# A hybrid decoder trunk: the inversion's small products in eight groups, Silu on ScalarE, and the norm's two steps moved

## The chip, the cores and the metric

The kernel runs on one core of one Trainium2 chip. The metric is the device time of one execution in microseconds (us). A core has five engines that run side by side and wait for each other by semaphores: TensorE (PE, matrix products; PEld is its weight load), VectorE (DVE), ScalarE (ACT), GpSimd (POOL) and SyncE (SP, which starts DMA transfers). Products land in PSUM, which has eight banks here called by tags; everything else is in SBUF.

## The reference

A trunk of DEPTH = 2 layers over 512 tokens of width 1024. Cut to what matters:

```python
for l in range(DEPTH):
    h = modulate(x, norm_ffn1[l], sh1, sc1)              # RMSNorm, scale, shift
    x = x + 0.5 * (1 + g1) * swiglu(h, ffn1_w1[l], ffn1_w3[l], ffn1_w2[l])
    h = modulate(x, norm_mix[l], sh2, sc2)
    x = x + (1 + g2) * token_mix(h, ...)                 # gated delta rule and MLA side by side
    h = modulate(x, norm_ffn2[l], sh3, sc3)
    x = x + 0.5 * (1 + g3) * swiglu(h, ffn2_w1[l], ffn2_w3[l], ffn2_w2[l])

def rms_norm(x, gain):
    return x * rsqrt(mean(x * x, -1) + EPS) * gain

def gated_deltanet(qkv, z, ...):
    q, k, v = split(silu(causal_dwconv(qkv, conv_w)))    # q, k: l2_norm per head
    ...
    t_inv = triangular_solve(eye + m, eye)               # m strictly lower, one per chunk and head
    ...
    return rms_norm(o, out_gain) * silu(z)

def mla(q_lat, kv_lat, ...):
    q = rms_norm(q_lat, q_lat_gain) @ w_q_up             # q_lat: 384 wide, kv_lat: 256 wide
    kv = rms_norm(kv_lat, kv_lat_gain) @ w_kv_up
    ...
```

Eight heads of width 128 in both mixers. The kernel works in chunks of 128 tokens, so per layer there are 8 x 4 = 32 triangular matrices of 128x128 to invert.

## The kernel before

Everything is held transposed: features on the 128 partitions, tokens along the free axis. A projection in float32 is made of three products in the faster fp32r format (`mm3`, L123): the high part of the weight by the high part of the activation, high by low, and low by high. A weight slab of 128x1024 comes in by DMA (`raw`), ACT casts it to the high part (`whi`, L119), and DVE subtracts to get the low part (`wlo`, L120). A **k-step** is three products of 128x128 by 512 columns; a **unit** is one slab, eight k-steps into one PSUM tile `acc`, and what is done with the result.

The mixer (`mix`) keeps a list of such units. Wherever a chain of small dependent work runs, `fill(n)` (L159) puts n k-steps of the queued units between its steps, so that PE has something to do. `FILL_INVERT`, `FILL_DELTA` and others say how many after which step. The order of the instructions on each engine is fixed when the program is built, by a list scheduler that goes by the program's order and by which instructions it takes to be ready; afterwards each engine runs its list strictly in order.

Places that the change and the prediction touch:

- `conv` (L498): the causal convolution of a head's q, k or v on ACT (L503) and DVE (L506), then Silu as a tanh on ACT (L508) and a DVE product (L509). Its result is twice the Silu; factors that make up for this are in `gdn_tail` (`4.0 * EPS`, `self.ogh`) and in `mix` (`nh`).
- `gdn_units` (L695): the units of a head's q, v and z. The z unit has its own tanh (L711) and DVE product (L713), which reads the `acc` tile.
- `latent_units` (L801): five units for the latents of MLA. Each squares its result (L811, into a `cv` buffer) and adds it (L815); the last unit of each kind then sums over the partitions by four products with a matrix of ones into an `sm` tile, and DVE makes the mean of it (L826).
- `invert` (L617): the 32 matrices at once. Each is cut in 32x32 blocks. DVE transposes the diagonal blocks (L629) and inverts them by 31 steps of substitution (L635, L637), in seven parts, each followed by 12 k-steps. Then L642 and L643 transpose the result to `xd` and `yd`; the tag `L` has five buffers, and `yd` gets its place in SBUF from those. Then come the **small products**: from the 32x32 inverses the 64x64 ones, from these the 128x128 ones, by products of 32x32 (160 per layer) and of 64x64 (64 per layer) in plain float32, each of which the profile shows as two records, 448 in all. They come in four stretches, with 8 k-steps behind each of the first three. The results are taken out of PSUM (`sm`, `sc`) by DVE and ACT copies.
- `gdn_chunk` and `gdn_tail` (L783): the delta rule itself and its output norm, which takes its root by `rsqrt`.
- `rsqrt` (L313): with a table, a Sqrt on ACT, a reciprocal and one Newton step on DVE; without, a first guess by integer arithmetic and three Newton steps, all on DVE.
- `norm_scale` (L328) makes an RMSNorm's factor in two steps: products with ones and the root; then a product that broadcasts the factor over the partitions (into `po`). `norm_apply` (L356) makes the next activations of it.
- `close` (L379) ends each half step: the output projection's slabs and their residual (L376), and on the way the sum of squares (`norm_square`, L301, whose L310 and L311 keep the running sum in `g`). The last four slabs are done once for the first 256 tokens (PSUM tag `acc`) and once for the second 256 (`sc`). The first half's norm is taken a step further after the residual of slabs 1 and 3 of the second half (`NORM_AT`). Its slabs have 8 k-steps after the mixer and up to 8 in the feed-forward parts, the last piece of whose inner width has 6.

Of the kernel before, what the change touches and what calls it, by code (L numbers as in the profile page):

```python
# [11 lines left out]
AF = mybir.ActivationFunctionType  # L12
# [27 lines left out]

FILL_INVERT = (12, 12, 12, 12, 12, 12, 12, 8, 8, 8)
FILL_DELTA = ((0, 2, 2), (2, 2, 2), (2, 2, 2), (2, 2, 2))
# [31 lines left out]
class Trunk:  # L74
    def __init__(self, ctx, tc, aps):
        self.tc = tc
        self.nc = tc.nc
        self.ap = aps
        self.sb = ctx.enter_context(tc.tile_pool(name="sb", bufs=1))
        self.ps = ctx.enter_context(tc.tile_pool(name="ps", bufs=1, space=bass.MemoryType.PSUM))  # L80
        self.count = 0
        self.pin = False
        self.units, self.body, self.ahead = [], None, None
        self.queue = []

    def order(self, i):
# [72 lines left out]
    def fill(self, n):  # L159

        for _ in range(n):
            while True:
                if self.body is None:
                    if not self.units:
                        return
                    load, body = self.units.pop(0)
                    self.body = body(self.ahead or load())
                    self.ahead = self.units[0][0]() if self.units else None
                if next(self.body, 0) != 0:
                    break  # L170
                self.body = None

    def fill_all(self):
        while self.units or self.body:
            self.fill(1)

    def hacts(self):
# [150 lines left out]
    def norm_scale(self, cols):  # L328
# [8 lines left out]
        nc.vector.tensor_scalar(var, ps[:, :, 0], 1.0 / D, EPS, ALU.mult, ALU.add)  # L337
        self.rsqrt(rn, var, True)
        yield
# [39 lines left out]
    def close(self, get, acts, gate, finish, spare=(), ahead=None):  # L379
# [15 lines left out]
        for (a, b), tag in zip(HALVES if ws else (), ("acc", "sc")):  # L395
            for m, s in zip(range(late, KT), ws):
                ps = self.p(tag)
                self.proj(ps, s, acts, (a, b))
                self.residual(m, ps, gate, (a, b))
                norm = finish(m, (a, b))  # L400
                if norms and m - late in NORM_AT:
                    next(norms[0], None)
                if norm is not None:
                    norms.append(norm)
# [92 lines left out]

    def conv(self, ps, vec, tile_index, out):  # L498

# [4 lines left out]
        for j in range(3):  # L504
            s = 3 - j
            nc.vector.scalar_tensor_tensor(acc[:, s:], ps[:, :SEQ - s], w[j], acc[:, s:], ALU.mult, ALU.add)  # L506
        th = self.t("cv", [P, SEQ])
        nc.scalar.activation(th, acc, AF.Tanh, scale=0.5)  # L508
# [108 lines left out]
    def invert(self, mall, tt):  # L617
# [13 lines left out]
        for j in range(B - 1):  # L631
# [6 lines left out]
            if j % 5 == 4:  # L638
# [6 lines left out]
        x64 = [self.t("O", [P, 16, 64]) for _ in range(2)]  # L645
        QUADS = [(slice(16 * i, 16 * i + 16), 16 * i, slice(a * B, (a + 1) * B), slice((a + 1) * B, (a + 2) * B), i, a)
                 for a in (0, 2) for i in range(2)]
        tags = ("sm", "sc")
        for ns, n0, sa, sb_, i, a in QUADS:
            ps = self.p(tags[i], [P, 16, B])  # L650
            for n in range(16):
                self.mm(ps[sb_, n, :], mall[sa, n0 + n, sb_], xd[sa, n0 + n, :], start=True, stop=True)
            nc.vector.tensor_copy(pq[sb_, ns, :], ps[sb_])
        for b in range(4):
            bs = slice(b * B, (b + 1) * B)
            nc.scalar.copy(tt[bs, :, bs], yd[bs])
        for i in range(2):
            ns = slice(16 * i, 16 * i + 16)
            nc.gpsimd.memset(x64[i][0:B, :, B:], 0.0)
            nc.scalar.copy(x64[i][0:B, :, 0:B], xd[0:B, ns, :])  # L660
            nc.scalar.copy(x64[i][B:2 * B, :, B:], xd[B:2 * B, ns, :])
        yield
        for ns, n0, sa, sb_, i, a in QUADS:
            if a == 0:
                ps3 = self.p(tags[i], [P, 16, B])
                for n in range(16):
                    self.mm(ps3[sb_, n, :], yd[sb_, n0 + n, :], pq[sb_, n0 + n, :], start=True, stop=True)
                nc.scalar.activation(x64[i][sb_, :, 0:B], ps3[sb_], AF.Copy, scale=-1.0)
        for ns, n0, sa, sb_, i, a in reversed(QUADS):
            ps2 = self.p(tags[i], [P, 16, B])  # L670
            for n in range(16):
                self.mm(ps2[sa, n, :], pq[sb_, n0 + n, :], yd[sb_, n0 + n, :], start=True, stop=True)
            nc.scalar.activation(tt[sa, ns, sb_], ps2[sa], AF.Copy, scale=-1.0)
        yield
        p2 = [self.t("O", [P, 16, 64]) for _ in range(2)]
        for i in range(2):
            for q in range(2):
                ps = self.p(tags[q], [P, 8, 64])
                for n in range(8):
                    m = 16 * i + 8 * q + n  # L680
                    self.mm(ps[64:, n, :], mall[0:64, m, 64:], x64[i][0:64, 8 * q + n, :],
                                     start=True, stop=True)
                nc.vector.tensor_copy(p2[i][64:, 8 * q:8 * q + 8, :], ps[64:])
        yield
        for i in range(2):
            for q in range(2):
                ps2 = self.p(tags[q], [P, 8, 64])
                m0 = 16 * i + 8 * q
                for n in range(8):
                    self.mm(ps2[0:64, n, :], p2[i][64:, 8 * q + n, :], tt[64:, m0 + n, 64:],  # L690
                                     start=True, stop=True)
                nc.scalar.activation(tt[0:64, m0:m0 + 8, 64:], ps2[0:64], AF.Copy, scale=-1.0)


    def gdn_units(self, l, h, vec, st):  # L695
# [4 lines left out]
        def qv(i, w):  # L700
            if i == 0:
                st["qv"] = self.t("O", [P, 2, SEQ])
            ps = self.p("acc")
            yield from self.proj_steps(ps, w, acts)
            self.conv(ps, vec, (h, 16 + h)[i], st["qv"][:, i, :])

        def z(w):
            ps = self.p("acc")
            yield from self.proj_steps(ps, w, acts)
            zt = self.t("cv", [P, SEQ])  # L710
            nc.scalar.activation(zt, ps, AF.Tanh, scale=0.5)  # L711
            st["z2"] = self.t("c3", [P, SEQ])
            nc.vector.scalar_tensor_tensor(st["z2"], zt, 1.0, ps, ALU.add, ALU.mult)  # L713

# [67 lines left out]

    def gdn_tail(self, st):  # L783

        nc = self.nc
        ssq, osb, z2 = st["ssq"], st["osb"], st["z2"]
        a, m = st["sso"], self.t("som", [P, NT])
        nc.vector.tensor_scalar(ssq, ssq, 4.0 * EPS, EPS * P, ALU.add, ALU.mult)
# [7 lines left out]
        nc.vector.scalar_tensor_tensor(z2, ot, self.ogh, z2, ALU.mult, ALU.mult)  # L796
        o = self.t("O", [P, 2, SEQ], F32R)
        self.split(o[:, 0, :], o[:, 1, :], z2)
        st["o"] = (o[:, 0, :], o[:, 1, :])

    def latent_units(self, l, vec, ms, out):  # L801
# [5 lines left out]
        def unit(i, w):  # L807
# [196 lines left out]
    def mix(self, l, vec, gate, finish, ws, ahead):  # L1004
# [21 lines left out]
        for h in range(2):  # L1026
            self.conv(pp[1 + h], vec, 8 + h, kT[h])
        for h in range(2, HEADS):
# [3 lines left out]
            self.key_system(l, gt, h - 2, kT[h - 2], mall)  # L1032
            self.conv(ps, vec, 8 + h, kT[h])
        heads = [{} for _ in range(HEADS)]
# [12 lines left out]
        nh = gt["nh"]  # L1047
        nc.vector.tensor_scalar(nh, gt["ssk"], 0.25, EPS, ALU.mult, ALU.add)
        rs = self.t("s1", [P, NI])
        self.rsqrt(rs[:], nh[:])  # L1050
        nc.vector.tensor_mul(nh, nh, rs)
        self.ogh = self.t("ogh", [P, 1])
        nc.vector.tensor_scalar(self.ogh, vec[:, V_OG:V_OG + 1], 0.5, None, ALU.mult)
        tt = self.t("A", [P, NI, P])
# [18 lines left out]
        for h in range(HEADS):  # L1073
            prep = self.gdn_prep(l, h + 1, gt, kT[h + 1], heads[h + 1]) if h + 1 < HEADS else iter(())
            for c in range(NT):
                for i, _ in enumerate(self.gdn_chunk(h, c, gt, kT[h], tt, heads[h])):
# [4 lines left out]
                    self.fill(FILL_DELTA[c][i])  # L1081
            tail = self.gdn_tail(heads[h])
            next(tail)
# [319 lines left out]
```

## Time and profile before

| | |
|---|---|
| median of 3 runs | 2811.39 us (2811.04 to 2812.45) |
| profiled execution | 2812.29 us |
| its span in the profile | 2810.4 us |
| PE busy | 2761.9 us, 98% |
| DVE busy | 1736.9 us, 62% |
| ACT busy | 1130.3 us, 40% |
| POOL busy | 156.4 us, 6% |
| DMA | 339.2 MB, mean 121 GB/s |

Times in the profile are in us from the start of the span, unless they are marked ns. A group row names the source line, engine, operation, output tile, inputs and count. A wait row names who waited for whom, the total, the number of times and the longest. The granted clock (PEclk) is the share of the full TensorE clock, 1.00 at most; the profile gives it in windows of 3.41 us. A busy PE is not the same as a PE at its pace: a small product and a product at half the clock both count as busy.

### The profile page before, as it was taken

What the parts mean: (1) busy time and instruction counts of PE and PEld (TensorE: products, weight loads), DVE (VectorE), ACT (ScalarE), POOL (GpSimd) and SP (SyncE); (2) the same over time, 40 slices, a digit from 0 to 9 for tenths busy, and PEclk for the clock granted to TensorE, in tenths of its full rate; (3) what the DMA queues carried; (4) which work ended last, traced back from release to release, by engine and by line L of the source; (5) the groups of instructions that cost most, each with busy time, mean ns of one, the idle gap of its engine ahead of it and who ended that gap; (6) DMA issues with size and microseconds to landing.
All of it is one profiled execution on the core that took longest, in us unless ns stands there. A gap on an engine that the chain in (4) does not pass through costs nothing. (4 is left out here: it accounts for less than half of the span.)

```text
span 2810.4 us, 38435 instructions
## 1 busy us (share of the span) xinstructions
PE 2761.9 (98%) x14648; PEld 2338.5 (83%) x14648; DVE 1736.9 (62%) x3677; ACT 1130.3 (40%) x2343; POOL 156.4 (6%) x238
## 2 busy tenths in 40 slices
PE   7999999999999999999999999999999999999999
PEld 6888888788888788888888888887888888988888
DVE  6555569867668755543456554797766786653333
ACT  3322255445546534222342222544555564432322
POOL 0000003000001010000000000130000111000000
PEclk9999999899999999999999999999999999999999
DMA  7556433222122343643336663332222223443332
GB/s 275 184 185 200 153 108 108 83 64 79 59 91 65 117 165 113 201 144 98 99 97 194 192 198 116 112 106 66 76 83 77 71 79 109 143 135 98 98 94 94
DMA packets 103720, 339.20 MB, mean 121 GB/s; under 512 B 11760, under 2 KB 14448, under 8 KB 103536
## 3 DMA queue, kind: packets, MB, share of 16 engines
q1 hardware_dynamic: 101088, 332.03, 37.2%
q10 hardware_dynamic: 2448, 4.72, 0.4%
q8 instruction: 115, 1.88, 0.3%
q14 instruction: 69, 0.57, 0.1%
HBM read 321.50 MB, written 15.20 MB: 120 GB/s over the span
## 5 line engine op out<-in xcount | busy, mean ns | idle before, releaser
L119 ACT CAST whi<-raw 128x512 fp32r<-128x512 f32 (+1 forms) x834 | 484.9, 611 | 1131.1 <-PE acc L92 535.2
L120 DVE TENSOR_TENSOR wlo<-raw,whi 128x512 fp32r<-128x512 f32 (+1 forms) x834 | 573.4, 708 | 244.6 <-ACT whi L119 236.6
L92 PE MATMUL acc<-hhi,whi 128*128 128x512 f32 (+1 forms) x1648 | 648.3, 394 | 3.2 <-DVE c L713 1.7
L92 PE MATMUL acc<-hlo,whi 128*128 128x512 f32 (+1 forms) x1648 | 628.0, 381 | 1.5 <-POOL hlo L370 1.5
L92 PE MATMUL acc<-hhi,wlo 128*128 128x512 f32 (+1 forms) x1648 | 628.6, 382 | 0.0
L92 PEld LDWEIGHTS acc<-hhi,wlo 128*128 128x128 f32 x1648 | 312.9, 190 | 59.8 <-DVE wlo L1230 0.4
L92 PEld LDWEIGHTS acc<-hhi,whi 128*128 128x128 f32 x1648 | 313.6, 191 | 53.2 <-DVE c L713 2.5
L92 PEld LDWEIGHTS acc<-hlo,whi 128*128 128x128 f32 x1648 | 314.2, 191 | 51.7 <-POOL hlo L370 2.5
L92 PE MATMUL acc<-O,whi 128*128 128x512 f32 x1088 | 335.8, 390 | 0.0
L92 PE MATMUL sc<-hhi,whi 128*128 128x512 f32 (+1 forms) x712 | 272.8, 383 | 0.0
L92 PE MATMUL sc<-hhi,wlo 128*128 128x512 f32 (+1 forms) x712 | 272.5, 383 | 0.0
L92 PE MATMUL sc<-hlo,whi 128*128 128x512 f32 (+1 forms) x712 | 272.3, 382 | 0.0
L92 PEld LDWEIGHTS acc<-O,whi 128*128 128x128 f32 x1088 | 203.5, 188 | 41.6
L428 DVE TENSOR_TENSOR g<-g,sc 128x512 f32<-128x512 f32 x87 | 59.8, 688 | 261.6 <-PE sc L92 256.8
L92 PE MATMUL acc<-O,wlo 128*128 128x512 f32 x544 | 211.9, 390 | 0.0
L376 DVE SCALAR_TENSOR_TENSOR M<-acc,gate,M 128x512 f32<-128x512 f32 (+1 forms) x112 | 77.5, 692 | 197.9 <-PE acc L92 191.4
L92 PE MATMUL acc<-A,whi 128*128 128x512 f32 x640 | 197.1, 389 | 0.0
L256 DVE SCALAR_TENSOR_TENSOR L<-L,L 128x1024 f32<-128x1024 f32 x142 | 169.4, 1218 | 0.2 <-DMA L<-in_ada_w 0.2
L92 PEld LDWEIGHTS sc<-hhi,wlo 128*128 128x128 f32 x712 | 134.2, 188 | 27.4 <-DVE wlo L120 1.3
L92 PEld LDWEIGHTS sc<-hlo,whi 128*128 128x128 f32 x712 | 134.0, 188 | 26.0
L92 PEld LDWEIGHTS sc<-hhi,whi 128*128 128x128 f32 x712 | 134.1, 188 | 25.8
L92 PEld LDWEIGHTS acc<-A,whi 128*128 128x128 f32 x640 | 120.1, 188 | 25.0
(373 smaller groups left out, 3725.2 us busy)
## 6 DMA issues: line engine op xcount, KB each, us to landing
raw<-in_ffn_w SPq DMA_DIRECT2D x236, 512.0 KB, 3.6
L<-in_ada_w SPq DMA_DIRECT2D x142, 512.0 KB, 4.6
raw<-in_w_in SPq DMA_DIRECT2D x108, 512.0 KB, 3.6
raw<-in_ffn_w SPq DMA_DIRECT2D x32, 384.0 KB, 3.2
raw<-in_w_branch_a SPq DMA_DIRECT2D x16, 512.0 KB, 3.5
raw<-in_w_branch_b SPq DMA_DIRECT2D x16, 512.0 KB, 3.6
raw<-in_w_out SPq DMA_DIRECT2D x16, 512.0 KB, 3.5
spill<-M SPq DMA_DIRECT2D x16, 256.0 KB, 2.0
```

The costliest lines, as they stand in the source:

```text
L92: i = self.nc.tensor.matmul(*a, **k)
L119: nc.scalar.copy(hi[:, s], raw[:, s])
L120: nc.vector.tensor_sub(lo[:, s], raw[:, s], hi[:, s].bitcast(F32))
L256: self.order(self.nc.vector.scalar_tensor_tensor(raw, raw, 1.0, self.condb, ALU.mult, ALU.mult, accum_out=mod[:, o:o + 1]))
L376: self.nc.vector.scalar_tensor_tensor(self.x[:, m, a:b], ps[:, a:b], gate[:, m:m + 1], self.x[:, m, a:b], ALU.mult, ALU.add)
L428: nc.vector.tensor_mul(s, s, ps3)
```

## The change

Five edits in one step.

1. The small products of the inversion come in nine groups with three k-steps between (eight gaps of 3, in place of three of 8). Within a group, products of two row blocks of the array alternate: blocks 0 and 2 in the first two groups, 1 and 3 in the next two; in the eighth group the upper and the lower half. The copies of `xd` and `yd` come behind the second group.
2. Silu is one ACT operation for q, v and z; the keys keep tanh and product. The factors 0.25, 0.5 and 4 that belonged to the doubled values go or move.
3. The root in `norm_scale` and in `gdn_tail` is taken without table, on DVE.
4. The latents' sum over the partitions is put on a list (`self.waiting`) and issued 14 k-steps later.
5. In `close` the two steps of the first half's norm come inside slab 1 and slab 3 of the second half, after 3/8 of its k-steps, rather than after the residual.

```diff
-FILL_INVERT = (12, 12, 12, 12, 12, 12, 12, 8, 8, 8)
+FILL_INVERT = (12, 12, 12, 12, 12, 12, 12) + (3,) * 8
...
                 if next(self.body, 0) != 0:
+                    self.count_down()
                     break
...
+    def count_down(self):
+        for w in list(self.waiting):
+            w[0] -= 1
+            if w[0] == 0:
+                self.waiting.remove(w)
+                w[1]()
...
-        self.rsqrt(rn, var, True)
+        self.rsqrt(rn, var, False)
...
-                self.proj(ps, s, acts, (a, b))
+                n = len(acts)
+                cut = 3 * n // 8 if norms and m - late in NORM_AT else n
+                self.proj(ps, s, acts, (a, b), range(cut))
+                if cut < n:
+                    next(norms[0], None)
+                    self.proj(ps, s, acts, (a, b), range(cut, n))
                 self.residual(m, ps, gate, (a, b))
                 norm = finish(m, (a, b))
-                if norms and m - late in NORM_AT:
-                    next(norms[0], None)
...
+        if not twice:
+            nc.scalar.activation(out, acc, AF.Silu)
+            return
         th = self.t("cv", [P, SEQ])
         nc.scalar.activation(th, acc, AF.Tanh, scale=0.5)
         nc.vector.scalar_tensor_tensor(out, th, 1.0, acc, ALU.add, ALU.mult)
...
-        for ns, n0, sa, sb_, i, a in QUADS:
+        for i, ns, n0 in halves:
             ps = self.p(tags[i], [P, 16, B])
             for n in range(16):
-                self.mm(ps[sb_, n, :], mall[sa, n0 + n, sb_], xd[sa, n0 + n, :], start=True, stop=True)
-            nc.vector.tensor_copy(pq[sb_, ns, :], ps[sb_])
+                for ra, rb in ((r0, r1), (r2, r3)):
+                    self.mm(ps[rb, n, :], mall[ra, n0 + n, rb], xd[ra, n0 + n, :], start=True, stop=True)
+            for rb in (r1, r3):
+                nc.vector.tensor_copy(pq[rb, ns, :], ps[rb])
...
+            yield
+        outs = []
+        for i, ns, n0 in halves:
+            ps2, ps3 = self.p(tags[i], [P, 16, B]), self.p(tags[i], [P, 16, B])
+            outs.append(ps2)
+            for n in range(16):
+                self.mm(ps3[r1, n, :], yd[r1, n0 + n, :], pq[r1, n0 + n, :], start=True, stop=True)
+                self.mm(ps2[r2, n, :], pq[r3, n0 + n, :], yd[r3, n0 + n, :], start=True, stop=True)
+            nc.scalar.activation(x64[i][r1, :, 0:B], ps3[r1], AF.Copy, scale=-1.0)
+            nc.scalar.activation(tt[r2, ns, r3], ps2[r2], AF.Copy, scale=-1.0)
+            yield
...
+        for i, ns, n0 in halves:
+            for n in range(16):
+                self.mm(outs[i][r0, n, :], pq[r1, n0 + n, :], yd[r1, n0 + n, :], start=True, stop=True)
+            nc.scalar.activation(tt[r0, ns, r1], outs[i][r0], AF.Copy, scale=-1.0)
+            yield
+        for q in range(2):
+            ps = self.p(tags[q], [P, 8, 64])
+            for n in range(8):
+                low(0, q, n, ps)
+            store_low(0, q, ps)
         yield
...
+        for q in range(2):
+            pl, ph = self.p(tags[q], [P, 8, 64]), self.p(tags[q], [P, 8, 64])
+            for n in range(8):
+                low(1, q, n, pl)
+                high(0, q, n, ph)
+            store_low(1, q, pl)
+            store_high(0, q, ph)
         yield
...
+        for q in range(2):
+            ps = self.p(tags[q], [P, 8, 64])
+            for n in range(8):
+                high(1, q, n, ps)
+            store_high(1, q, ps)
...
-            zt = self.t("cv", [P, SEQ])
-            nc.scalar.activation(zt, ps, AF.Tanh, scale=0.5)
-            st["z2"] = self.t("c3", [P, SEQ])
-            nc.vector.scalar_tensor_tensor(st["z2"], zt, 1.0, ps, ALU.add, ALU.mult)
+            st["z"] = self.t("c3", [P, SEQ])
+            nc.scalar.activation(st["z"], ps, AF.Silu)
...
-        self.rsqrt(m[:], a[:])
+        self.rsqrt(m[:], a[:], False)
...
-                s = self.p("sm", [P, NT, P])
-                for c in range(NT):
-                    self.mm(s[:, c, :], keep["sq"][:, c * P:(c + 1) * P], self.ones, start=True, stop=True)
                 which = 0 if i < QL else 1
-                n = (QL, KL)[which] * P
-                nc.vector.tensor_scalar(ms[:, which, :], s[:, :, 0], 1.0 / n, EPS, ALU.mult, ALU.add)
+                sq = keep["sq"]
+                self.waiting.append([14, lambda: mean(which, sq)])
```

`low` and `high` are the 64x64 products of the lower and upper half, `store_low` and `store_high` their copies out of PSUM (DVE and ACT); `mean` does what the lines taken from `unit` did.

More of the change, by code (lines that the diff above doesn't have):

```diff
@@ L84, in __init__ @@
         self.queue = []
+        self.waiting = []
     def order(self, i):
@@ L169, in fill @@
                 if next(self.body, 0) != 0:
+                    self.count_down()
                     break
                 self.body = None
+    def count_down(self):
[4 more added lines that the diff above has]
+                w[1]()
     def fill_all(self):
-        while self.units or self.body:
+        while self.units or self.body or self.waiting:
             self.fill(1)
+            if not (self.units or self.body):
+                self.count_down()
     def hacts(self):
@@ L495, in ffn, with conv @@
         down(2)
-    def conv(self, ps, vec, tile_index, out):
+    def conv(self, ps, vec, tile_index, out, twice):
         nc = self.nc
@@ L645, in invert @@
         x64 = [self.t("O", [P, 16, 64]) for _ in range(2)]
-        QUADS = [(slice(16 * i, 16 * i + 16), 16 * i, slice(a * B, (a + 1) * B), slice((a + 1) * B, (a + 2) * B), i, a)
-                 for a in (0, 2) for i in range(2)]
+        halves = [(i, slice(16 * i, 16 * i + 16), 16 * i) for i in range(2)]
+        r0, r1, r2, r3 = (slice(b * B, (b + 1) * B) for b in range(4))
         tags = ("sm", "sc")
-        for ns, n0, sa, sb_, i, a in QUADS:
+        for i, ns, n0 in halves:
             ps = self.p(tags[i], [P, 16, B])
@@ L651, in invert @@
             for n in range(16):
-                self.mm(ps[sb_, n, :], mall[sa, n0 + n, sb_], xd[sa, n0 + n, :], start=True, stop=True)
-            nc.vector.tensor_copy(pq[sb_, ns, :], ps[sb_])
[L654 to L661, printed above, removed]
@@ L662, in invert @@
-        yield
[L663 to L673, printed above, removed]
@@ L674, in invert @@
-        yield
[L675 to L692, printed above, removed]
+                for ra, rb in ((r0, r1), (r2, r3)):
+                    self.mm(ps[rb, n, :], mall[ra, n0 + n, rb], xd[ra, n0 + n, :], start=True, stop=True)
@@ new lines, in invert @@
+            for rb in (r1, r3):
+                nc.vector.tensor_copy(pq[rb, ns, :], ps[rb])
+            if i:
+                for b in range(4):
+                    bs = slice(b * B, (b + 1) * B)
+                    nc.scalar.copy(tt[bs, :, bs], yd[bs])
+                for j, js, _ in halves:
+                    nc.gpsimd.memset(x64[j][0:B, :, B:], 0.0)
+                    nc.scalar.copy(x64[j][r0, :, 0:B], xd[r0, js, :])
+                    nc.scalar.copy(x64[j][r1, :, B:], xd[r1, js, :])
@@ new lines, in invert, with low, high, store_low @@
+        p2 = [self.t("O", [P, 16, 64]) for _ in range(2)]
+        def low(i, q, n, ps):
+            self.mm(ps[64:, n, :], mall[0:64, 16 * i + 8 * q + n, 64:], x64[i][0:64, 8 * q + n, :], start=True,
+                    stop=True)
+        def high(i, q, n, ps):
+            m = 16 * i + 8 * q + n
+            self.mm(ps[0:64, n, :], p2[i][64:, 8 * q + n, :], tt[64:, m, 64:], start=True, stop=True)
+        def store_low(i, q, ps):
+            nc.vector.tensor_copy(p2[i][64:, 8 * q:8 * q + 8, :], ps[64:])
@@ new lines, in store_high @@
+        def store_high(i, q, ps):
+            m0 = 16 * i + 8 * q
+            nc.scalar.activation(tt[0:64, m0:m0 + 8, 64:], ps[0:64], AF.Copy, scale=-1.0)
+        for i, ns, n0 in halves:
[8 more added lines that the diff above has]
+            store_low(0, q, ps)
@@ L704, in qv @@
             yield from self.proj_steps(ps, w, acts)
-            self.conv(ps, vec, (h, 16 + h)[i], st["qv"][:, i, :])
+            self.conv(ps, vec, (h, 16 + h)[i], st["qv"][:, i, :], False)
         def z(w):
@@ L781, in gdn_chunk, with gdn_tail @@
         yield
-    def gdn_tail(self, st):
+    def gdn_tail(self, vec, st):
         nc = self.nc
-        ssq, osb, z2 = st["ssq"], st["osb"], st["z2"]
+        ssq, osb, z = st["ssq"], st["osb"], st["z"]
         a, m = st["sso"], self.t("som", [P, NT])
-        nc.vector.tensor_scalar(ssq, ssq, 4.0 * EPS, EPS * P, ALU.add, ALU.mult)
+        nc.vector.tensor_scalar(ssq, ssq, EPS, EPS * P, ALU.add, ALU.mult)
         nc.vector.scalar_tensor_tensor(a, a, 1.0 / P, ssq, ALU.mult, ALU.add)
-        self.rsqrt(m[:], a[:])
+        self.rsqrt(m[:], a[:], False)
         nc.vector.tensor_mul(osb, osb, m[:].unsqueeze(2).to_broadcast([P, NT, P]))
@@ L795, in gdn_tail @@
             self.tr(ot[:, c * P:(c + 1) * P], osb[:, c, :], self.ident)
-        nc.vector.scalar_tensor_tensor(z2, ot, self.ogh, z2, ALU.mult, ALU.mult)
+        nc.vector.scalar_tensor_tensor(z, ot, vec[:, V_OG:V_OG + 1], z, ALU.mult, ALU.mult)
         o = self.t("O", [P, 2, SEQ], F32R)
-        self.split(o[:, 0, :], o[:, 1, :], z2)
+        self.split(o[:, 0, :], o[:, 1, :], z)
         st["o"] = (o[:, 0, :], o[:, 1, :])
@@ L820, in unit, with mean @@
             if i in (QL - 1, QL + KL - 1):
-                s = self.p("sm", [P, NT, P])
-                for c in range(NT):
-                    self.mm(s[:, c, :], keep["sq"][:, c * P:(c + 1) * P], self.ones, start=True, stop=True)
                 which = 0 if i < QL else 1
-                n = (QL, KL)[which] * P
-                nc.vector.tensor_scalar(ms[:, which, :], s[:, :, 0], 1.0 / n, EPS, ALU.mult, ALU.add)
+                sq = keep["sq"]
+                self.waiting.append([14, lambda: mean(which, sq)])
+        def mean(which, sq):
+            s = self.p("sm", [P, NT, P])
+            for c in range(NT):
+                self.mm(s[:, c, :], sq[:, c * P:(c + 1) * P], self.ones, start=True, stop=True)
+            n = (QL, KL)[which] * P
+            nc.vector.tensor_scalar(ms[:, which, :], s[:, :, 0], 1.0 / n, EPS, ALU.mult, ALU.add)
         return [(lambda i=i: self.win(l, WLAT + i), lambda w, i=i: unit(i, w)) for i in range(QL + KL)]
@@ L1026, in mix @@
         for h in range(2):
-            self.conv(pp[1 + h], vec, 8 + h, kT[h])
+            self.conv(pp[1 + h], vec, 8 + h, kT[h], True)
         for h in range(2, HEADS):
@@ L1032, in mix @@
             self.key_system(l, gt, h - 2, kT[h - 2], mall)
-            self.conv(ps, vec, 8 + h, kT[h])
+            self.conv(ps, vec, 8 + h, kT[h], True)
         heads = [{} for _ in range(HEADS)]
@@ L1047, in mix @@
         nh = gt["nh"]
-        nc.vector.tensor_scalar(nh, gt["ssk"], 0.25, EPS, ALU.mult, ALU.add)
+        nc.vector.tensor_scalar(nh, gt["ssk"], 4.0 * EPS, None, ALU.add)
         rs = self.t("s1", [P, NI])
@@ L1051, in mix @@
         nc.vector.tensor_mul(nh, nh, rs)
-        self.ogh = self.t("ogh", [P, 1])
-        nc.vector.tensor_scalar(self.ogh, vec[:, V_OG:V_OG + 1], 0.5, None, ALU.mult)
         tt = self.t("A", [P, NI, P])
@@ L1081, in mix @@
                     self.fill(FILL_DELTA[c][i])
-            tail = self.gdn_tail(heads[h])
+            tail = self.gdn_tail(vec, heads[h])
             next(tail)
```

## The prediction

> **What bounds the kernel now.** I read the page first (busy shares, the chain of work that ended last), then the waits of TensorE (PE) alone, then tables of windows, and last the timeline of the few places where PE is not at its pace. The first fence is the pace (chain of waits), the second PE's waits: releaser, total us, times, longest.
>
> ```profile
> 2545.22 48.96 PE acc L92 x216
> ```
> ```profile
> PE sm L92 <- DVE cv L815: 7.8, 2, 3.9
> ...
> PE sm L92 <- DVE g L311: 5.5, 5, 1.1
> ...
> PE acc L92 <- DVE c L713: 1.7, 2, 0.9
> ```
> The third is windows: stretch, length, busy time (and instructions) of PE, PEld, DVE, ACT, POOL, then granted clock, DMA share, GB/s. The span comes first, then per layer the *long stage* (seven fills of 12 k-steps beside the substitution) and the *group stage* (the inversion's small products with their 24 k-steps).
>
> ```profile
> 0.00:2810.40 2810.40, 2761.95 (x14648) 2338.52 (x14648) 1736.86 (x3677) 1130.32 (x2343) 156.44 (x238) 0.99 0.38 121
> ...
> 476.83:543.00 66.17, 61.52 (x263) 50.20 (x261) 62.78 (x131) 24.91 (x43) 7.66 (x12) 0.95 0.29 88
> 1867.42:1932.60 65.18, 60.34 (x263) 49.13 (x261) 62.94 (x131) 24.81 (x43) 7.89 (x12) 0.97 0.28 89
> 542.94:582.86 39.92, 39.88 (x521) 34.38 (x521) 21.32 (x31) 18.45 (x29) 0.00 (x0) 0.87 0.19 61
> 1932.60:1972.45 39.85, 39.81 (x521) 34.36 (x521) 21.30 (x31) 18.45 (x29) 0.00 (x0) 0.87 0.20 61
> ```
> PE is busy for 2762 of 2810 us and a 128x512 product takes 48.96/216 = 0.2267 us. So nothing off PE is worth anything unless PE waits for it, runs at a lower clock, or runs products that fill little of the array. The diff takes away no PE instruction. All it can gain lies in four places: the three waits above, the clock (0.95, 0.97, 0.87, 0.87 where the span has 0.99), and the pace of the small products. In the long stage VectorE (DVE) is as tight as PE: 62.78 busy of 66.17 us.
>
> **The change part by part**
>
> *(a, b) The long stage: Silu on ScalarE, and the latents' ones-products 14 k-steps later.* The tile view of `cv`, the window rows of L509 and of L713 alone (DVE busy, count), and windows in which the clock stood at 0.50:
>
> ```profile
> L509 DVE SCALAR_TENSOR_TENSOR O<-cv,cv x2: 682/684/686, 515.7 to 521.5; 128x512 f32<-128x512 f32 x2
> L503 ACT ACTIVATE cv<-acc,vec x1: 689/689/689, 516.5 to 516.5; 128x512 f32<-128x512 f32 x1
> L811 ACT ACTIVATE cv<-acc x1: 597/597/597, 522.3 to 522.3; 128x512 f32<-128x512 f32 x1
> L815 DVE TENSOR_TENSOR cv<-cv,cv x1: 680/680/680, 523.4 to 523.4; 128x512 f32<-128x512 f32 x1
> ```
> ```profile
> 476.83:543.00 66.17, 3.44 (x5) 0.95 0.29 88
> 476.83:543.00 66.17, 2.05 (x3) 0.95 0.29 88
> ```
> ```profile
> 523.28:530.11 6.83, 5.91 (x18) 5.07 (x19) 5.11 (x15) 1.62 (x3) 0.00 (x0) 0.50 0.38 126
> 547.17:550.59 3.42, 3.42 (x11) 2.73 (x9) 3.36 (x4) 0.56 (x1) 0.00 (x0) 0.50 0.03 7
> 557.41:564.24 6.83, 6.83 (x63) 5.44 (x60) 0.69 (x1) 2.88 (x5) 0.00 (x0) 0.50 0.26 79
> ```
> The square of the last latent (L811, 522.3) gets its `cv` buffer only after the convolution's last DVE operation (L509, until 522.2); L815 ends at 524.06 and the ones-products, first in PE's order, stand 3.9 us for it. Right after, the clock is 0.50 for 6.83 us. Fourteen k-steps are 42 x 0.2267 = 9.5 us, over twice the 3.9, so the wait goes, and with it the clock's fall. The Silu removes the five L509 and three L713 in this stage, 3.44 + 2.05 = 5.49 us of DVE, and with them the wait of 1.7 at L713. ACT has room: 24.9 of 66 us.
>
> What is late next? PE's floor is 252 x 0.2267 = 57.1, with some 1.1 for the ones-products (eight records of the kind that takes 0.60 for four at 392.48, below): 58.2. DVE has 62.78 - 5.49 = 57.3 left; if it keeps its present idle time (66.17 - 62.78 = 3.4) the stage takes 60.7, since the small products need the DVE transposes at its end (L642, L643). I take the middle, 59.4, as both engines are equally loaded: 66.17 - 59.4 = 6.8 and 65.18 - 59.4 = 5.8, **-12.6**; bounds -15.0 (58.2 twice) and -10.0 (60.7 twice).
>
> *(c) The groups.* Same 24 k-steps and same 448 small records per layer; four stretches become nine, with three k-steps (2.0 us) between; and products of two row blocks alternate. The PE timeline where the small products begin, then around the 64x64 ones; last, windows with the `acc` products (the k-steps) alone:
>
> ```profile
> 543.15 1.17 PE L92 MATMUL sm<-L,M 32*32 32x32 f32 x32
> 544.15 1.08 PE L92 MATMUL sc<-L,M 32*32 32x32 f32 x29
> 545.05 0.21 PE L92 MATMUL sm<-L,M 32*32 32x32 f32 x1
> 545.07 0.19 PE L92 MATMUL sc<-L,M 32*32 32x32 f32 x1
> 545.10 0.19 PE L92 MATMUL sm<-L,M 32*32 32x32 f32 x1
> 545.10 0.19 PE L92 MATMUL sc<-L,M 32*32 32x32 f32 x1
> ```
> ```profile
> 569.13 0.39 PE L92 MATMUL acc<-hhi,wlo 128*128 128x512 f32 x1
> 569.45 1.14 PE L92 MATMUL sm<-O,M 64*64 64x64 f32 x16
> ...
> 573.32 0.50 PE L92 MATMUL acc<-hhi,whi 128*128 128x512 f32 x1
> 573.66 0.39 PE L92 MATMUL acc<-hlo,whi 128*128 128x512 f32 x1
> ```
> ```profile
> 554.00:557.41 3.41, 0.50 (x3) 0.07 (x1) 1.49 (x2) 0.00 (x0) 1.00 0.42 154
> 571.07:574.48 3.41, 1.16 (x5) 0.99 (x6) 0.75 (x1) 0.00 (x0) 1.00 0.02 5
> ```
> 32 records of 32x32 start within 1.00 us: 0.0313 each. The burst of 64 records of 64x64 costs, from one undisturbed k-step to the next, (573.66 - 0.227) - (569.13 + 0.227) = 4.07 us: 64 x 0.0584 and 0.33 for switching. Today per layer: k-steps 72 x 0.2267 = 16.3; small 320 x 0.0313 + 128 x 0.0584 = 17.5; five switches 1.65; the rest, 39.9 - 35.45 = 4.45, is the half clock (at most half of 3.42 + 6.83 us, 5.1, so it fits).
>
> Where the stream passes from one row block to the other (545.05 to 545.10: sm, sc, sm, sc) starts come 0.02 to 0.03 apart: the two overlap. It is a stretch of a few records, and it has two banks. Overlapped throughout, the new order takes 256 x 0.0313/2 (first four groups) + 64 x 0.0313 (two groups of one block) + 64 x 0.0584 (first and last 64x64 group) + 64 x 0.0584/2 = 11.6. If the two groups whose pairs share one PSUM tile do not overlap, 13.6; nothing overlapped, 17.5. I take 12.6, between the first two, as the one row shown is of overlap.
>
> The clock fell after windows with almost no k-step in them (0.50 us of `acc` in 554.00:557.41) and not after one with 1.16 (34%). In the new stage three k-steps (2.0 us) follow at most 2.3 us of small products, so any 3.41 us hold over 1.1 us of them; I take it that the clock stays. The order of today's stretches shows that the built order follows the program here. After: 16.3 + 12.6 + 9 x 0.33 = 31.9, and 0.5 for a wait at the first group, because PE now reaches `xd` (L642) earlier while `yd` (L643) takes the same buffer only after the second group: 32.4. That is -7.5 per layer, **-15.0**. Bounds: 30.9 (full overlap, no wait), -18.0; with no overlap and one window at half clock (17.5 instead of 12.6, and 1.7), 39.0, -1.8.
>
> *(d) Norm in the close; norm roots on DVE.* PE's rows at the end of a close, and the DVE row that the first moved step needs:
>
> ```profile
> 387.74 0.50 PE L92 MATMUL sm<-ones,g 128*128 128x1 f32 x4
> 388.10 4.54 PE L92 MATMUL sc<-O,A 128*128 128x256 f32 x36
> 392.48 0.60 PE L92 MATMUL po<-const,nv 128*128 128x128 f32 x4
> 394.19 0.61 PE L92 MATMUL sm<-ones,g 128*128 128x1 f32 x4 [1.10 <-DVE g L311]
> ```
> ```profile
> 386.46 0.43 DVE L311 TENSOR_TENSOR g<-g,g 128x256 f32<-128x256 f32 x1 [0.55 <-ACT g L310]
> ```
> Today the broadcast (`po`, 392.48) comes when the last slab has ended, so the next stage's first products cannot start before the second half's ones-product at 394.19: PE stands 1.1 us, five times. With the broadcast at 3/8 of the last slab the first half's activations are ready some 1.3 us sooner (18 products in (392.48 - 388.10)/2 = 2.2 us; 5/8 of them), and they cover most of the wait: I take -0.9 each, **-4.5** (best 1.3 each, -6.5). Against it: the first step comes at 387.74 - 1.3 = 386.4 while its sum is ready at 386.9, and a wait there would sit in front of the slab in PE's order: at worst +0.7 five times, +3.5. Between -6.5 and +3.5 I stay near the measured wait.
>
> ```profile
> L325 DVE TENSOR_TENSOR nr<-nr,nv 128x2 f32<-128x2 f32 x10 | 1.6, 161 | 0.3
> ```
> The root without table is six DVE operations more, 6 x 0.16 = 1.0 us, and one operation fewer on ACT, for which I count nothing; it has the rest of two slabs (over 4 us) to hide in. Without that cover it would cost 1 us at each of five norms; that lies inside the bound.
>
> *(e) The rest*: key convolutions keep Tanh; the eight tails lie in the delta stage beside PE's work: 0 +-1.5.
>
> Sum: -12.6 - 15.0 - 4.5 = -32.1, against the profiled run's 2812.29 (its span is 2810.4, 1.9 lie around it): **2780.2**. That run lies 0.9 above the median of 2811.39, which leaves 2779.3; I say **2780**. Bounds added: -41 (2771) and -6.8 (2805.5).
>
> **The rivals**
>
> *No overlap in the array.* If alternating row blocks run no faster, the small products stay at 17.5: +4.9 per layer, 2790. For it: only some eight records show overlap. Against: those. Two milder forms stay in my own case. If same-bank pairs run one after the other, 13.6: 2782. If a start never comes sooner than 25 ns, 6.4 for the first four groups instead of 4.0: S = 14.0, 2783.
>
> The Trainium skill, "TensorEngine Tiling (Array Packing)", section "Gotcha 1: PSUM Pressure", says that different row tiles cannot access the same PSUM bank simultaneously; the first two groups do just that, and by this rule 13.6 holds for them. The Trainium skill, "TensorE: Matmul & The Clock Gate", section "Wait — 56ns, not 53.3ns?", puts the least start-to-start at about 25 ns; the rows at 545.05 to 545.10 have starts 17 ns apart on average, over too few records to speak against it.
>
> *The clock falls all the same, or the groups run together*: the wait for `xd` or `yd` makes a window with few k-steps, or the built order puts two groups next to each other (the change then not doing what it says). One to three windows of 3.41 us per layer at half clock, at most 1.7 each: +3.4 to +10, and with a wait of 1 us each up to 2797.
>
> *Little gained*: the overlap fails, the long stage is held by DVE at 60.7 and the norm's moved step waits: 2797 to 2806.
>
> *Slower: the clock falls at the first group and never returns within the stage.* In 557.41:564.24 the clock stayed low through two windows although k-steps were among the small products. Of the new stage k-steps are 16.3/32.4 = 50% throughout. If the clock needs more than that to come back, the whole stage runs at half: +16.3 + 12.6 = +28.9 per layer, 61.3 instead of 39.9. With the gains of (a, b) and (d): 2780.2 + 57.8 = 2838. It decides from the point where one wait of about 3 us at the first group empties a window.
>
> **How the numbers follow.** My case (2773 to 2786, with both milder forms) 0.58; below it 0.02; no overlap (2786 to 2793) 0.15; clock or order (2789 to 2797) 0.12; little gained (2797 to 2806) 0.06; within 0.2% of before, about what a measurement of this kernel can tell from no change (2806 to 2817), 0.03; slower (about 2838) 0.04. Faster is 0.93. The range from 2770 to 2797 leaves about 0.13 out, all but little of it above.
>
> **What would show it.** Right: granted clock 1.00 in both group stages and no half-clock window at the latents; no wait of PE for L815 or L713; small groups starting under 25 ns per record where blocks alternate; group stages of about 32 us and long stages of about 59; the five waits on L311 gone. Wrong: 0.50 anywhere in a group stage; starts 31 ns apart in alternating groups; PE waiting for DVE's `L` tiles before the first group, or at the norm's moved ones-product.

## The result and the profile after

| | before | changed |
|---|---|---|
| median | 2811.92 us (4 runs, 2811.04 to 2815.74) | 2794.71 us (4 runs, 2793.02 to 2795.32) |
| ratio, 95% interval | | 0.9935 (0.9918 to 0.9952) |
| profiled execution | 2812.29 us, span 2810.4 | 2795.32 us, span 2793.5 |

The changed kernel is faster by 17 us, where 32 were forecast. That is inside the stated range (2770 to 2797) but outside the likeliest case (2773 to 2786, chance 0.58); it lies where the rival of the clock was put (2789 to 2797, chance 0.12). The waits of PE in the changed kernel (line numbers there are higher: L662 is the transpose to `yd`, L138 the split of a latent, L323 the sum of squares):

```profile
PE sm L93 <- DVE L L662: 5.8, 2, 2.9
PE acc L93 <- DVE L L138: 3.2, 2, 1.6
PE acc L93 <- POOL hlo L382: 2.4, 8, 0.3
...
PE sm L93 <- DVE g L323: 1.2, 3, 0.7
```

And its windows: long stage and group stage of each layer, then the two stretches at half clock.

```profile
476.92:537.00 60.08, 58.51 (x263) 48.02 (x261) 58.60 (x122) 23.39 (x40) 7.64 (x12) 1.00 0.29 88
537.00:573.93 36.93, 34.03 (x522) 27.50 (x521) 19.29 (x27) 20.92 (x33) 0.00 (x0) 0.91 0.26 80
1860.17:1920.30 60.13, 58.52 (x263) 48.01 (x261) 58.65 (x122) 23.38 (x40) 7.65 (x12) 1.00 0.28 88
1920.30:1956.82 36.52, 33.65 (x522) 27.16 (x521) 19.26 (x27) 20.91 (x33) 0.00 (x0) 0.91 0.25 81
546.91:553.74 6.83, 6.83 (x109) 5.44 (x110) 3.77 (x6) 5.79 (x7) 0.00 (x0) 0.50 0.28 79
1929.31:1936.14 6.83, 6.04 (x75) 4.68 (x77) 4.61 (x7) 6.38 (x8) 0.00 (x0) 0.50 0.23 78
```

The three waits that the forecast named first (the latents' sum, the z unit, five norm waits of 1.1) are gone or smaller. In their place stands one that it had priced at 0.5: 2.9 us per layer for `yd`, with 6.83 us at half clock right behind it. The borders of these windows cut the span into seven stretches, and the difference of each says where the time went:

| stretch | before | changed | difference |
|---|---|---|---|
| start to the first long stage | 476.83 | 476.92 | +0.1 |
| long stage, layer 1 | 66.2 | 60.1 | -6.1 |
| group stage, layer 1 | 39.9 | 36.9 | -3.0 |
| from there to the second long stage | 1284.6 | 1286.2 | +1.7 |
| long stage, layer 2 | 65.2 | 60.1 | -5.1 |
| group stage, layer 2 | 39.85 | 36.5 | -3.3 |
| the rest | 838.0 | 836.7 | -1.3 |

Two things are to be explained: the group stages gave 6.3 us instead of 15, and the stretches with the norms gave nothing where 4.5 were counted.

How the wait comes about is in the timeline of three engines in layer 1. First PE (around the first group, then the third), then ACT, then DVE:

```profile
536.76 0.39 PE L93 MATMUL acc<-hhi,wlo 128*128 128x512 f32 x1
537.08 1.20 PE L93 MATMUL sm<-L,M 32*32 32x32 f32 x64
538.21 0.50 PE L93 MATMUL acc<-hhi,whi 128*128 128x512 f32 x1
538.54 0.40 PE L93 MATMUL acc<-hlo,whi 128*128 128x512 f32 x1
...
543.54 0.39 PE L93 MATMUL acc<-hhi,wlo 128*128 128x512 f32 x1
546.83 0.18 PE L93 MATMUL sm<-O,L 32*32 32x32 f32 x1 [2.90 <-DVE L L662]
```
```profile
542.18 0.63 ACT L524 ACTIVATE O<-cv 128x512 f32<-128x512 f32 x1 [1.90 <-DVE cv L522]
542.82 0.62 ACT L683 COPY O<-L 32x512 f32<-32x512 f32 x1
543.45 0.62 ACT L682 COPY O<-L 32x512 f32<-32x512 f32 x1
544.08 0.62 ACT L683 COPY O<-L 32x512 f32<-32x512 f32 x1
```
```profile
540.56 1.52 DVE L522 SCALAR_TENSOR_TENSOR cv<-acc,vec,cv 128x510 f32<-128x510 f32 x2
542.12 1.40 DVE L675 COPY O<-sm 32x512 f32<-32x512 f32 x2
543.54 0.68 DVE L675 COPY O<-sc 32x512 f32<-32x512 f32 x1
544.73 1.96 DVE L662 STREAM_TRANSPOSE L<-L 128x1024 f32<-128x1024 f32 x1 [0.51 <-ACT O L683]
```

The last copies that read `xd` (L682, L683) stand on ACT behind a Silu (L524), which waits for the convolution on DVE. Only after the last of them, at 544.70, may the transpose write `yd` into the place of `xd`; PE had come to the third group at 543.77. ACT's copies are only the last link: DVE itself was busy with the convolution and the first groups' copies until 544.22, stood 0.51 us for ACT, and then the transpose takes 1.96 us.

### The profile page after: what moved, and what is told of

The parts are those of the page before. It is cut to its first block, busy times and chain, and to the rows that moved or that the text cites. A ratio compares the mean times of both kernels' runs of the same rounds, so it can differ in the third digit from the quotient of the medians.

```text
span 2793.5 us, 38452 instructions
## 1 busy us (share of the span) xinstructions
PE 2750.2 (98%) x14648; PEld 2321.8 (83%) x14648; DVE 1729.9 (62%) x3783; ACT 1081.2 (39%) x2283; POOL 154.6 (6%) x238
## 4 chain that ended last, share of the span: by engine, by line
PE 84%; DVE 9%; ACT 3%; DMA 2%; issue 1%; POOL 0%; SPq 0%; ACTq 0%; DVEq 0%; POOLq 0%
PE acc L93 56%; PE sc L93 23%; DVE wlo L121 2%; PE sm L98 2%; PE sm L93 2%; PE po L93 1%; DVE cv L522 1%; DMA raw<-in_ffn_w 1%; DVE L L654 1%; DMA raw<-in_w_in 1%; DVE L L656 1%; DVE L L648 1%; ACT whi L120 1%; ACT hhi L379 0%; DVE mx L1019 0%
```

## The experiments

Runs of the kernel before stand beside them (medians 2809.9 to 2811.7). Each is an edit of the changed kernel.

**1. `yd` in a place of its own.** The two halves of `yd` receive the elements in another arrangement; the work and the dependences are those of the kernel.

```diff
-        yd = self.t("L", [P, NI, B])
+        yd = [self.t("g", [P, 16, B]) for _ in range(2)]
```

> yd goes to two g tiles and waits for nobody who reads xd. In the changed kernel TensorE waits 2.90 us per layer at the third group for yd's transpose, and a stretch of 6.83 us at half clock begins at the same time. Theory A (the wait for yd's buffer empties a clock window): wait and half-clock stretch both go, the group stage falls from 36.9 and 36.5 us to about 30.6 (2.9 for the wait, half of 6.83 for the clock), 2795 falls to about 2782. Rival B (the small products alone lower the clock): the wait goes, half-clock windows stay, about 2789. Rival C (VectorE is short here whatever yd waits for): the wait moves to the copies of the first groups, group stage 35 or more, 2792 or more.

2790.51 us. The group stages of layers 1 and 2:

```profile
537.60:572.30 34.70, 32.91 (x521) 26.40 (x521) 19.49 (x29) 20.06 (x35) 0.00 (x0) 0.95 0.30 93
1920.45:1952.22 31.77, 31.44 (x522) 25.56 (x521) 18.07 (x28) 19.33 (x33) 0.00 (x0) 0.99 0.30 100
```

The wait for L662 is gone, but in layer 1 PE then waits for the copies of the first products (1.8 us), because these stand on DVE behind convolutions that wait for ACT. The clock also stood at 0.50 for 3.41 us in each layer. The total lies between the theories: layer 2 comes near A, layer 1 is as C has it. The place of `yd` is one link; the queues of ACT and DVE just then are another.

**2. No alternation within a group.**

```diff
-            for n in range(16):
-                for ra, rb in ((r0, r1), (r2, r3)):
+            for ra, rb in ((r0, r1), (r2, r3)):
+                for n in range(16):
...
```

> Same nine groups and gaps, but within a group all products of one row block come before those of the other. Theory A (alternating row blocks overlap in the array, 15 ns per record instead of 31): the first four groups take 1.0 us more each and the eighth 1.9 more, 5.9 per layer; up to 2 us of it is given back because the wait for yd gets shorter: 2803 to 2807. Rival B (the record pitch does not depend on the order): same time as the changed kernel, 2794 to 2796.

2799.35 us, 4.6 more, between the two expected ranges (four runs, 2796.66 to 2804.07). The profile is of the slowest of them. Its group stages (the clock fell for 13.65 us in layer 1 and not at all in layer 2):

```profile
538.11:581.16 43.05, 41.92 (x521) 34.62 (x520) 19.43 (x27) 20.91 (x33) 0.00 (x0) 0.84 0.21 69
...
1928.39:1965.52 37.13, 36.01 (x521) 30.18 (x521) 19.43 (x27) 20.92 (x33) 0.00 (x0) 1.00 0.24 79
```

Layer 2, at full clock and less its wait of 1.1 for `yd`, takes 36.0 us; the same groups with alternation take 31.0 (experiment 5). So the overlap is worth 5.0 us per layer, near the 5.9 expected by A; the total rose by less, in part because the wait for `yd` shrank from 2.9 to 1.1 us.

**3. The norm's steps in their old place. 4. The root with the table.** First the edit of 3, then that of 4:

```diff
-                cut = 3 * n // 8 if norms and m - late in NORM_AT else n
...
+                if norms and m - late in NORM_AT:
+                    next(norms[0], None)
```
```diff
-        self.rsqrt(rn, var, False)
+        self.rsqrt(rn, var, True)
```

> The two steps of the first half's norm come again after the residual of slabs 1 and 3; the root stays without table. Between the start of the last close of ffn1 and the long stage the changed kernel lost 2.45 us against before in layer 1 and 2.0 in layer 2. Theory A (the moved steps cost: three waits of 0.74 at the ones-product, and the second half's ones come later): 3 to 5 us of it come back, 2790 to 2792. Rival B (the root's ten operations in series make the second half late): no gain, 2794 to 2797.

2793.59 us, 1.1 less, which is within the spread of the changed kernel's own runs (2793.02 to 2795.32); in the profiled run the half-clock stretch of layer 1 was 3.41 instead of 6.83 us long, which alone is over 1 us. Theory A fails.

> The root in the norm uses the Sqrt table again; the moved steps stay. Theory B (the root without table makes the second half late): waits of TensorE for the broadcast's factor (0.9 us, 5 times together) and the late second half go, 3 to 5 us less, 2790 to 2792. Rival A (the moved steps do it): no gain, 2794 to 2797.

2788.23 us, 6.5 less. Theory B, and by more than it said, but not all of it is the root's: in the profiled run 2.6 us lie in the second layer's group stage, where PE waits 1.4 instead of 2.9 us for `yd`. Experiments 5 and 9, in which that wait is gone, give 5.8 us for the root. The root of the second half's norm on DVE, in the changed kernel and in this one, from its first operation after the mean to its last:

```profile
398.69 0.17 DVE L333 TENSOR_SCALAR nv<-nv 128x2 int32<-128x2 int32 x1
...
400.46 0.16 DVE L338 SCALAR_TENSOR_TENSOR nv<-nr,nv 128x2 f32<-128x2 f32 x1
```
```profile
399.93 0.17 DVE L331 RECIPROCAL nv<-nv 128x2 f32<-128x2 f32 x1 [0.27 <-ACT nv L330]
...
400.52 0.16 DVE L338 SCALAR_TENSOR_TENSOR nv<-nr,nv 128x2 f32<-128x2 f32 x1
```

1.9 us against 0.8 (and 0.3 of waiting for ACT's Sqrt before it). Part of what it costs shows at the products that follow, which wait for the activations' low parts less often with the table:

```profile
PE acc L93 <- POOL hlo L382: 1.0, 3, 0.3
```

The lists of PE's instructions differ too, since the order is made again for each kernel. How the rest divides between the longer chain and the other order was not measured.

**5. More cover before the third group.**

```diff
-FILL_INVERT = (12, 12, 12, 12, 12, 12, 12) + (3,) * 8
+FILL_INVERT = (12, 12, 12, 12, 12, 12, 12) + (3, 8, 3, 2, 2, 2, 2, 2)
```

> The changed kernel with gaps of 3, 8, 3, 2, 2, 2, 2, 2 k-steps in place of eight times 3: five k-steps more (5 x 0.68 = 3.4 us) stand before the third group, where TensorE waits 2.90 us for yd. Theory A (the wait, and with it the empty clock window, is all that the group stage lost): the wait is 0 to 0.3, no half-clock stretch, group stage 30 to 31.5 instead of 36.9 and 36.5, 2782 to 2785. Rival B (with two k-steps, 1.4 us, between small groups the clock falls there): wait gone, half-clock windows in the later groups, 2787 to 2791. Rival C (the engines' queues shift with the k-steps, so the wait stays): 2793 or more.

2784.92 us, 9.8 less. Long and group stages:

```profile
477.11:537.18 60.07, 58.45 (x263) 48.02 (x261) 58.59 (x122) 23.40 (x40) 7.66 (x12) 1.00 0.28 88
537.18:568.17 30.99, 30.99 (x521) 25.23 (x520) 19.29 (x27) 20.93 (x33) 0.00 (x0) 1.00 0.31 96
1854.44:1914.54 60.10, 58.46 (x263) 48.02 (x261) 58.62 (x122) 23.39 (x40) 7.72 (x12) 1.00 0.28 88
1914.54:1945.53 30.99, 30.99 (x521) 25.23 (x520) 19.29 (x27) 20.93 (x33) 0.00 (x0) 1.00 0.30 95
```

This settles the group stage: PE is busy all of it, the clock stays at 1.00, no wait for `yd` is left, and 30.99 us is what the changed products take. The 36.93 of the changed kernel are those 31.0, 2.9 of wait and 3.0 of half clock.

**6. The old groups in the changed kernel** (the inversion's products and gaps as before).

> The changed kernel with the inversion's small products as before (four stretches, gaps of 8, row blocks one after the other). What the regrouping brought is the difference: by the stages 39.9 - 36.9 and 39.85 - 36.5, 6.3 us, so 2800 to 2802. If the waits in front of the stage are longer with the earlier arrival, up to 2 us more; if the regrouping brought nothing by itself (all of it from Silu and the delayed ones-products), 2794 to 2796.

2802.38 us, just above the expected 2800 to 2802: the regrouping is worth 7.7 us as it stands.

**7. Tanh and product for q, v and z again. 8. The ones-products at once.**

> The changed kernel with tanh and a VectorE product for q, v and z again. VectorE gets 5.49 us more in each long stage. Theory A (VectorE sets the long stage's length now): 60.1 becomes 64 to 65.6, the total 2803 to 2806. Rival B (TensorE's k-steps set it, 58.2 us, and VectorE only where it waits): 60.1 to 62, 2795 to 2799.

2792.28 us, 2.4 *less* with the edit undone and below both expected ranges. Its long and group stages show why:

```profile
477.36:540.90 63.54, 60.27 (x263) 48.69 (x261) 62.64 (x131) 24.87 (x44) 7.72 (x12) 0.98 0.29 92
540.90:572.20 31.30, 31.19 (x522) 25.38 (x521) 21.28 (x30) 18.64 (x29) 0.00 (x0) 0.99 0.25 77
1859.13:1922.60 63.47, 58.92 (x263) 47.94 (x261) 62.58 (x131) 24.89 (x44) 7.73 (x12) 1.00 0.29 92
1922.60:1953.88 31.28, 30.98 (x521) 25.27 (x521) 21.26 (x30) 18.62 (x29) 0.00 (x0) 1.00 0.25 78
```

Without Silu the long stage is 3.4 us longer, and the group stage 5.4 shorter: the wait for `yd` does not occur, and the clock does not fall behind it. (In layer 1 it falls once for 3.41 us, where the long stage passes into the group stage.) The edit of experiment 8:

```diff
-                self.waiting.append([14, lambda: mean(which, sq)])
+                mean(which, sq)
```

> The changed kernel with the latents' ones-products right after the latent's unit, as before. Theory A (the delay took away the wait of 3.9 us per layer and the half-clock stretch behind it): with Silu the square is earlier, so a wait of 2 to 4 us per layer and 1.7 to 3.4 for the clock come back, 2801 to 2808. Rival B (the wait was due to the conv buffer that VectorE's product held, which Silu frees): no wait, 2794 to 2797.

2797.06 us, 2.4 more. The long stages are nearly as long as before the change:

```profile
478.44:544.66 66.22, 60.96 (x263) 50.09 (x261) 61.20 (x125) 26.26 (x45) 7.72 (x12) 0.95 0.28 88
1862.62:1927.95 65.33, 60.09 (x263) 49.51 (x261) 61.17 (x125) 26.27 (x45) 7.72 (x12) 0.95 0.27 89
```

The wait came back:

```profile
PE sm L93 <- DVE cv L856: 10.5, 2, 5.3
```

PE waits 5.3 us for the latent's square sum, and the clock falls for 6.83 us. Silu alone does not shorten the stage. This is theory A's mechanism, but the total ends at the edge of rival B's range, because the group stages shrink to 31.7 us each: PE comes later, and waits only 0.7 us for `yd`.

**9. Table and cover together. 10. In addition, the third latent's unit two units later. 11. Cover without Silu. 12. As 9, with the norm's old place.** What experiment 10 adds to 9:

```diff
-        units = [lat_units[0], lat_units[1], hu[0][2], hu[1][2], hu[0][0], hu[0][1], hu[1][0], hu[1][1], lat_units[2],
-                 hu[2][2], hu[2][0], hu[2][1]]
+        units = [lat_units[0], lat_units[1], hu[0][2], hu[1][2], hu[0][0], hu[0][1], hu[1][0], hu[1][1],
+                 hu[2][2], hu[2][0], lat_units[2], hu[2][1]]
```

> The two gains together on the changed kernel: gaps 3, 8, 3, 2, 2, 2, 2, 2 and the Sqrt table in the norm's root. By itself the first brought 9.8 us (2794.71 to 2784.92) and the second 6.5 (to 2788.23). Theory (they lie at different places and add up): 2777 to 2780. Rival (the gaps work only by the arrival times that the slower root gave): 2782 to 2785.

2779.12 us (ratio 0.9885, 0.9868 to 0.9901): the best version, 15.6 us below the changed kernel. The two gains add up.

> As the run before, and the third latent's unit two units later, so that its split no longer stands behind the transpose to xd on VectorE, for which TensorE waits 1.6 us per layer near the end of the long stage. Theory A (VectorE sets the long stage: its chain ends earlier without that unit's square sum and split): 60.1 becomes 58.3 to 59, 2 to 3.5 us less than the run before. Rival B (the work comes back in the group stage, where VectorE or the L buffers hold something else): within 1 us of the run before, or more.

2782.7 us, 3.6 more. PE at the first group:

```profile
532.64 0.39 PE L93 MATMUL acc<-hhi,wlo 128*128 128x512 f32 x1
535.68 1.20 PE L93 MATMUL sm<-L,M 32*32 32x32 f32 x64 [2.66 <-DVE L L661]
```

PE loses the wait for L138, arrives 2.7 us early, stands for `xd` instead, and the clock falls. So VectorE's chain sets the end of the long stage here: it ends at the same length (59.96 us) though PE had less to do in it.

> Gaps 3, 8, 3, 2, 2, 2, 2, 2 without Silu. Undone alone, Silu made the long stage 63.6 instead of 60.1 us, yet the total 2.4 us shorter, because the wait at the third group went. Theory A (Silu is worth its 3.5 us per layer once that wait is covered): 2784.92 + 7 = 2791 to 2793. Rival B (the regrouped products cost the same either way and Silu brings nothing): 2784 to 2786.

2792.68 us, 7.8 more than with Silu (2784.92): theory A. Not all of it is the long stage: in the profiled run (2796.38 us, the slowest of four) the clock also stands at 0.50 for 3.41 us in each group stage, after PE has waited for VectorE.

```profile
542.60:575.15 32.55, 32.47 (x521) 26.22 (x521) 21.39 (x30) 18.67 (x29) 0.00 (x0) 0.95 0.24 69
```

> The run with the table and the longer gap (2779.12), with the norm's two steps back in their old place: the norm is then that of before. With the slower root the move cost about 1 us (2794.71 against 2793.59). Theory A (with the fast root the move gains, by the stretches of the table run 1 to 2 us): 2780 to 2782. Rival B (the move costs by itself, the three waits of 0.7 at the ones-product): 2777 to 2778.5.

2781.7 us, 2.6 more than run 9. With the table, the moved steps gain 2.6 us; with the slower root they gained nothing (1.1 us lost, within the spread).

## Why the prediction was right or wrong

**(a, b) The long stage: right, size nearly so.** Forecast 59.4 us, measured 60.1 and 60.1; -11.1 instead of -12.6. DVE was busy for 58.6 us instead of the 57.3 counted, PE for 58.5, and the bound of 60.7, where DVE's chain sets the end, was the better guide than the middle. That the delayed ones-products take away wait and half clock is shown by experiment 8, that Silu shortens VectorE's chain by experiment 7. The wait at L713 went. The wait of 1.6 us for a latent's split (L138, behind the transpose to `xd`) took its place. Experiment 10 shows that nothing is gained by removing that wait alone, since PE then stands for `xd`.

**(c) The groups: the pace was right, the wait was mis-sized.** The forecast was 31.9 us of work and 0.5 of wait. The work is 30.99, the bound of full overlap (30.9): 64 records of the first group take, between undisturbed k-steps, (538.54 - 0.227) - (536.76 + 0.227) = 1.33 us, which less 0.33 is 15.6 ns per record, half of the 31 of one row block. The rival without overlap is out, and so are its two milder forms (31 ns for pairs in one PSUM tile, or 25 ns at least). The groups are nine, as counted, not the eight of the title. The failed term is "0.5 for a wait at the first group": the wait was at the third, for `yd`, and 2.9 us. I had seen that `yd` takes the place of `xd`, but counted only PE as a reader of `xd`. ACT's four copies read it as well, and their queue stood behind a Silu that waits for VectorE. Nor had I counted VectorE's own queue, busy until 0.45 us after PE's arrival, and the 1.96 us of the transpose itself, which are most of the wait. The second failed step is "I take it that the clock stays". It does stay in a stage of these groups (experiment 5, 1.00 throughout), but not after a gap of 2.9 us. The rival of the clock that falls at such a wait is what happened, with a wait of 2.9 us where it had 1: 5.9 us in layer 1 and 5.5 in layer 2 by the stage times. Less the 0.5 priced and the 0.9 that the groups ran faster, both per layer, that is the 8.7 us missing from the groups, more than half of the miss of 15. The clock came back within the stage, so the slower rival is out.

**(d) The norm: wrong sign.** Forecast -4.5. Over the same base, both norm edits together cost 2784.92 - 2781.7 = 3.2 us. That the root "has the rest of two slabs (over 4 us) to hide in" is the step that failed. It fits only the first half's root. The second half's root lacks that cover: its broadcast, and behind it the second half's activations, follow at once, and PE waits up to 0.2 us for it five times. Root without table: 5.8 us (2784.92 - 2779.12), over five norms 1.2 each, against the 1.0 that the text gave as the price if the cover is gone. That the second half's longer chain makes this up is inferred from the rows in experiment 4; the other order of PE's instructions was not separated from it. The move itself gains 2.6, within the bounds but short of 4.5; the wait at the moved ones-product that was named as its risk came as foreseen, 0.74:

```profile
384.85 0.61 PE L93 MATMUL sm<-ones,g 128*128 128x1 f32 x4 [0.74 <-DVE g L323]
```

**(e) The rest: 0 forecast, some 3 us of gain found.** The differences before the first long stage hide a gain of 2.3 at the very start and a loss of 2.4 around the first norm. The start differs by up to 1.9 us between changed kernels whose start is the same, so I do not put it down to the change. About 1 us per layer was gained where the delta stage passes into MLA. There PE had waited for POOL, and after the change this wait is not among PE's waits:

```profile
PE sm L97 <- POOL s L839: 2.4, 2, 1.2
```

No run took apart which edit removed it.

**The sum.** -32.1 forecast, -17.0 measured in the profiled runs: 8.7 from the groups, 7.7 from the norm by experiments 5 and 12, 1.5 from the long stage, against some 3 of unforeseen gain. That the range holds is owed to the rival of the clock, whose upper end is that of the range, and in part to luck, since the unforeseen gain hid some of the norm's loss. With the wait covered and the table kept, the same change gives 2779.1, which is the forecast, but that is another kernel: the agreement rests on two errors taken out and the unforeseen gain left in.

## What to carry to other kernels

An engine that is made faster arrives earlier, and what it then waits for is the price: before counting a gain, list every reader of each buffer that must come free next, on every engine, what stands ahead of them in that engine's queue, and how long the operation that refills the buffer takes. A work-filled gap is a margin, and should be put where the next dependence is late, not spread evenly. A chain of small operations is hidden only where other work can run meanwhile; the last one of a series, here the second half's norm, has less of it.

## What the runs showed of the hardware

Products of 32x32 in two row blocks overlap fully even when both write one PSUM tile (different partitions of it): 15.6 ns per record in the first group, against 31 for one block. I had put this between the two.

The clock fell after a window that PE left mostly empty, even for a wait of under 3 us. The windows of the changed kernel with the k-steps alone (the first and the last are followed by 0.50, the middle one is not):

```profile
543.50:546.91 3.41, 0.43 (x2) 0.01 (x1) 0.00 (x0) 0.68 (x1) 1.00 0.01 4
1915.66:1919.07 3.41, 1.80 (x8) 1.40 (x8) 1.48 (x2) 0.46 (x1) 1.00 0.01 2
1925.90:1929.31 3.41, 1.34 (x6) 0.75 (x4) 0.00 (x0) 0.68 (x1) 1.00 0.23 94
```

The forecast's sign, that 1.16 us of k-steps in a window are enough, did not carry over: there a burst of 64x64 products ran beside them, here 1.34 us beside an empty stretch were not enough. Where the windows lie against a wait seems to decide: in experiment 2 the same wait of 1.1 us was followed by 13.65 us at half clock in layer 1, where the window before held 0.75 us of k-steps, and by none in layer 2, where the window around the wait held 1.81. Part of the spread of the times of one kernel, some 2 us here, may come from this; that was not tested by itself.
